# The MLP over two halves of 528 tokens in quarters of 264 columns, all sixteen pairs by seven products

## The chip, the cores and the metric

The kernel runs on one core of one Trainium2 chip. The metric is the device time of one launch in microseconds (us), lower is better. Three runs of the kernel before gave 1785.30, 1794.46 and 1788.88 us, median 1788.88.

## The reference

One step of a hybrid encoder layer on 1024 prompt tokens and 32 tokens of a second request, 1056 in all, with D = 1024 and weights shared by both. In float32 throughout:

```python
h = rms_norm(x, g_mix); q, k, v, ch, cb, cc, ga, gb = split(h @ w_in)
x = x + (sigmoid(ga) * (attn(q, k, v) @ w_attn_out) + sigmoid(gb) * (cb * conv3(cc * ch) @ w_conv_out)) @ w_mix_out
cq = rms_norm(x, g_cross) @ w_cq                  # 4 heads of 64, 256 memory tokens
x = x + (softmax(cq mem_k / 8) mem_v) @ w_co
x = x + square(relu(rms_norm(x, g_mlp) @ w_up)) @ w_down      # w_up 1024 x 4096, w_down 4096 x 1024
y = rms_norm(x, g_final)
```

The last line but one, the MLP, is what the change rewrites.

## The kernel before

Activations are held transposed: a tile is 128 features (partitions) by tokens (columns), and `x1[c][f]` is slice f (of eight) of token chunk c. The three chunks `CH` have 384, 384 and 288 tokens. Every float32 product is three matmuls on values split in a high part (fp32r) and the rest: weight-high by activation-high, weight-high by activation-low, weight-low by activation-high (`gemm` L183 to L185, `product` L851 to L853, `part` L1586 to L1588). The weights are the 128x128 stationary operand and the tokens the moving one, so a matmul costs by its columns.

A weight of 512 KB (128 x 1024) is loaded by SyncE into `wr` (two buffers), cast on ScalarE to `wh` (L125) and the difference `wl` taken on VectorE (L126), with three buffers of `wh` and `wl` and two weights of lead (`LOOK`). SP issues nearly all DMAs, in the order in which the Python code runs. Work is laid down by hand as a list of items (`item`, `beside`): `beside` lays one step of a list (attention work) and some late calls after each filler. A weight in `kept` has its low part stored the first time (`wl_d`), and read back the second time. Instructions of an engine run in the order in which the built program has them; PSUM tiles `acc`, `pa` and `pq` are released by the engine that reads them.

The part that matters here comes after the mix projection of the last chunk:

- Cross-attention of chunk 2 goes in steps beside fillers (`cross_steps(2)`). Fillers are MLP products: the first eight of 32 slices of w_up by chunk 0, then the same eight by chunk 1 (`do_up`, 24 matmuls of 384 columns each, L183 to L185), then the same eight by chunk 2 (288 columns). `normed_split` makes the normalised operand of a chunk: a product with gain and `R[c]` (L1212), a write to `xn_d`, a cast (L1215) and a subtraction (L1216); R comes from the statistics (`chunk_stats`, L214 to L242), and of chunk 1 it comes while the fillers on chunk 0 run. `up_part` evicts a result: relu (L1240 or L1242), a square on GpSimd (L1244), a write of the hidden slice.
- `combine` (L1263 to L1273) makes the sums t2, n1, n3, n4 of the operands of chunk 0 and chunk 1, four features each, on VectorE, ScalarE and GpSimd, beside the products of chunk 2. They are the left operands of a Strassen-like scheme.
- The remaining 24 slices of w_up go as 12 pairs (`up_pair`). The tokens of chunks 0 and 1 are the two halves of the scheme, and a pair of weight slices gives the four results (two halves by two slices) in seven products of half the depth, instead of eight. `pair_issue` makes the weight sums on GpSimd (L1292 to L1295). Chunk 2 goes the plain way (`up_c2`, tile `pa`). Each pair takes 84 matmuls of 384 columns and 48 of 288. The results are combined on VectorE (h22 L1368 and L1369, u2 L1359, h12 L1378, h21 L1393, m3 and m2 at L1383 and L1386) and on GpSimd (n1 L1388, m4 L1396), squared (L1320) and stored in DRAM.
- `open_down` and the down projection: seven products per pair again on 384 columns for chunks 0 and 1, with chunk 2 plain beside them (`beside_two`, `alone`, `two`). Operands that the four plain fillers made are combined later by `refold` (reads, subtractions and writes of their own); operands come through `pump` (load, cast L781, subtraction L782) before they are due. `final` and `final_last` make the final norm and write the output.

The tail after the last product is the last chunk's addition, its statistics and transposes (L1636), and the scaling and writing of the transposed output (L1652, L1654).

Of the kernel before, what the change touches and what calls it, by code (L numbers as in the profile page):

```python
# [23 lines left out]
NF = 8  # L24
KV = 4
# [13 lines left out]
def hybrid_step(ctx: ExitStack, tc: tile.TileContext, io):  # L39
# [40 lines left out]
    xn_d = [dram.tile([P, NF, n], F32, name=f"xn_d{c}") for c, (_, n) in enumerate(CH[:2])]  # L80

    op_d = {k: dram.tile([P, 16, 384], F32, name=f"{k}_d") for k in ("b11", "b12", "b21", "b22", "n1", "n3", "t2", "n4")}
    hid2_d = dram.tile([P, 2, 16, 288], F32, name="hid2_d")
# [671 lines left out]
    def yslot(c):  # L755
        return slot(Y["pool" if c < 2 else "top"], f"Y{c}", CH[c][1])
# [11 lines left out]
    def open_y(*_):  # L768
        closed(A["cm"])
        closed(kv_cm)  # L770
        G["pool"] = ctx.enter_context(tc.tile_pool(name="gb", bufs=5, reuse_waits="tile", side="right"))
        Y["pool"] = ctx.enter_context(tc.tile_pool(name="ypool", bufs=16, reuse_waits="tile", side="right"))
        open_top()
# [91 lines left out]
    def close_gates():  # L865
        pump(0)
        assert not wanted
        closed(Y["cm"])
        open_top()
        ctx.push(Y["cm"])  # L870
# [124 lines left out]
    mpool = cr_cm = cr = None  # L995

    def after_gates():
        nonlocal mpool, cr_cm, cr
# [4 lines left out]
        mpool = ctx.enter_context(tc.tile_pool(name="mpool", bufs=16, reuse_waits="tile"))  # L1003
        cr_cm, cr = opened("cross", bufs=1, reuse_waits="tile")
# [7 lines left out]
    xm = [[None] * NF for _ in CH]  # L1012
# [160 lines left out]
    def do_co(c, half):  # L1173
        def fn(w):
# [3 lines left out]
            for f in fs:  # L1178
# [9 lines left out]
                if half == 0 and c == 2:  # L1188
                    xm[c][f] = gain_split(x, G_MLP + f, c)
                square_acc(x, f, c)  # L1190
            if half == 1 and c == 2:
                for f in fs:
                    xm[c][f] = gain_split(x1[c][f], G_MLP + f, c)
# [7 lines left out]
    L = {}  # L1201

    def open_late():
        closed(cr_cm)
        L["cm"], L["pool"] = opened("late", bufs=1, reuse_waits="tile")

    def lt(n=384):
        return L["pool"].tile([P, n], F32, tag="lt", bufs=6, name=nm("lt"))

    def normed_split(c, f):  # L1210
        t = tmp(CH[c][1])
        pin(dve.scalar_tensor_tensor(t, x1[c][f], col(G_MLP + f), R[c], op0=ALU.mult, op1=ALU.mult))  # L1212
        sp.dma_start(xn_d[c][:, f], t)
        hi, lo = xm[c][f] = (yslot(c), yslot(c))
        act.copy(hi, t)  # L1215
        pin(dve.tensor_sub(lo, t, hi.bitcast(F32)))  # L1216
# [12 lines left out]
    def hidden(c, j, h):  # L1229
        half, i = j % 8 // 4, j // 8 * 4 + j % 4  # L1230
        put(hid2_d[:, half, i] if c == 2 else op_d[f"b{half + 1}{c + 1}"][:, i], h)

    def up_part(w, c, j):
        n = CH[c][1]
        a = ps.tile([P, n], F32, tag="pt", bufs=2, name=nm("pa")) if w[0] == "late" else acc_tile([P, n])
        gemm(a, w[-2:], xm[c])
        flush()
        t = tmp(n)
        if c == 2:
            dve.scalar_tensor_tensor(t, a, 0.0, R[c], op0=ALU.max, op1=ALU.mult)  # L1240
        else:
            dve.tensor_scalar_max(t, a, 0.0)  # L1242
        h = tmp(n)
        pool_e.tensor_tensor(h, t, t, op=ALU.mult)  # L1244
        hidden(c, j, h)

    def do_up(j, c):
        return (lambda w: up_part(w, c, j)), ("w_up", j)
# [4 lines left out]
    def comb_slot(kind, k):  # L1253
        if kind in ("N1", "N3"):
            return mslot(384)
        return L["pool"].tile([P, 384], F32R, tag="hx", bufs=8, name=nm("hx")) if k < 2 else yslot(1)

    def combine(k):
        b12, b22, b11, b21 = (lt() for _ in range(4))
        for t, c, f in ((b12, 1, k), (b22, 1, k + 4), (b11, 0, k), (b21, 0, k + 4)):  # L1260
            sp.dma_start(t, xn_d[c][:, f])
        n3, n1, t2, n4 = b22, b12, b11, b21
        pin(dve.tensor_sub(n3, b12, b22))  # L1263
        pin(dve.tensor_sub(n1, b11, b12))
        pin(dve.tensor_sub(t2, b11, n3))
        pin(pool_e.tensor_tensor(n4, b21, t2, op=ALU.subtract))
        for kind, x in (("T2", t2), ("N1", n1), ("N3", n3), ("N4", n4)):
            hi, lo = comb[kind, k] = (comb_slot(kind, k), comb_slot(kind, k))
            act.copy(hi, x)
            if kind[0] == "T" or kind == "N1":  # L1270
                pin(dve.tensor_sub(lo, x, hi.bitcast(F32)))
            else:
                pin(pool_e.tensor_tensor(lo, x, hi.bitcast(F32), op=ALU.subtract))  # L1273
# [5 lines left out]
    def pair_fetch(key, src1, src2):  # L1279
        r1 = wp.tile([P, 1024], F32, tag="wr", bufs=2, name=nm("wr"))  # L1280
        r2 = L["pool"].tile([P, 1024], F32, tag="wr2", bufs=2, name=nm("wr2"))
        sp.dma_start(r1, src1)
        sp.dma_start(r2, src2)
        raws[key] = [r1, r2]

    def pair_issue(key, which):
        r1, r2 = raws[key][:2]
        a, b = slice(0, 512), slice(512, 1024)
        if which == 4:
            s31 = L["pool"].tile([P, 1024], F32, tag="s31", name=nm("s31"))  # L1290
            s24 = L["pool"].tile([P, 1024], F32, tag="s24", name=nm("s24"))
            pool_e.tensor_tensor(s31[:, b], r2[:, a], r2[:, b], op=ALU.add)  # L1292
            pool_e.tensor_tensor(s24[:, a], r1[:, a], s31[:, b], op=ALU.add)
            pool_e.tensor_tensor(s24[:, b], r1[:, b], s24[:, a], op=ALU.add)
            pool_e.tensor_tensor(s31[:, a], r1[:, a], r2[:, a], op=ALU.add)  # L1295
            raws[key] += [s31, s24]
        src = {1: 0, 2: 1, 3: 2, 4: 3}[which]
        if which == 2:
            hi, lo = (L["pool"].tile([P, 1024], F32R, tag=t, name=nm(t)) for t in ("wh2", "wl2"))
        else:  # L1300
            hi, lo = (wp.tile([P, 1024], F32R, tag=t, name=nm(t)) for t in ("wh", "wl"))
        split(hi, lo, raws[key][src])
        wset[key, which] = (hi, lo)

    UP = [(8 * g + i, 8 * g + i + 4) for g in range(1, 4) for i in range(4)]

    def up_fetch(i):
        if i < len(UP):
            pair_fetch(("u", i), io["w_up"][UP[i][0]], io["w_up"][UP[i][1]])

    def up_issue(i, which):
        if i < len(UP):
            pair_issue(("u", i), which)
        elif which != 2:
            if worder[wpos[0]] is STOP:
                wpos[0] += 1
            issue_w()

    def square_relu(v):
        dve.scalar_tensor_tensor(v, v, 0.0, v, op0=ALU.max, op1=ALU.mult)  # L1320
        return v

    b11, b21, b22 = (lambda k: xm[0][k]), (lambda k: xm[0][k + 4]), (lambda k: xm[1][k + 4])
    four = lambda get: [get(k) for k in range(4)]
    s1s, rs = {}, {}

    def up_w(i, which):
        return wset[("u", i), which]

    def up_p1(i):  # L1330

        A = acc_tile([P, 384])
        product(A, up_w(i, 1), 0, four(b11), True)
# [506 lines left out]
```

## Time and profile before

| | us |
|---|---|
| runs | 1785.30, 1794.46, 1788.88 (median 1788.88) |
| the profiled execution's span | 1791.7 |
| end of the last mix product, start of the fillers | 1057.2 |
| first matmul of the pairs | 1176.9 |
| first matmul of the down projection | 1435.6 |
| last addition of chunk 1 after the last product | 1779.4 |

Besides its span the profiled execution has no time of its own on the page; the span lies 2.8 us above the median of the runs and within their spread. One row of "lines" gives engine, operation, output and inputs, shapes and number of instructions, then the busy time and mean duration, then the idle time of that engine ahead of them. A window's row gives its length and each engine's busy time (instructions in parentheses), then the granted TensorE clock, the DMA engines' mean share, and GB/s. A row of the timeline gives the start, the duration, the engine, the line and the operation, with the idle time before it and its releaser in brackets. A matmul's own duration is longer than the distance to the next one, since they overlap; that distance is what counts. A row of DMA issues gives the queue's engine, number, size and the median us from issue to landing.

### The profile page before, as it was taken

The page shows a single profiled execution, that of the slowest core. Times are in us where ns is not written, and L with a number is a line of the kernel's source. Part 1 is how long each engine was busy: PE and PEld are TensorE (multiplying, and loading weights), DVE is VectorE, ACT ScalarE, POOL GpSimd, SP SyncE. Part 2 cuts the span into 40 slices and gives each one's busy share as a digit, 9 for nine tenths or more (in the row PEclk, how much of TensorE's full clock was granted, in tenths as well). Part 3 has the DMA queues.
Part 4 walks back from the last instruction along what each step waited for, and adds up shares of the span by engine and source line. Part 5 has one row for each costly group of instructions (what it writes and reads, how often), then busy time and mean ns, then how long its engine had stood idle before and what let it go on. Part 6 is the DMA issues. An engine that isn't in the chain of part 4 may idle for free. (4 is left out here: it accounts for less than half of the span.)

```text
span 1791.7 us, 30247 instructions
## 1 busy us (share of the span) xinstructions
PE 1754.1 (98%) x11110; PEld 1732.5 (97%) x11110; DVE 1173.1 (65%) x2165; ACT 799.6 (45%) x1566; POOL 594.2 (33%) x681
## 2 busy tenths in 40 slices
PE   8999999999999999999999989999999999999997
PEld 8999999999999999999999989999999999999997
DVE  6776767868666646546566777767566676436763
ACT  8643534435345334334565745632222343324453
POOL 0013146553453444511224142386554300100111
PEclk9999999999999999999999999999999999999999
DMA  5232234344346888758765657754333487446673
GB/s 181 98 116 92 87 104 153 118 142 144 137 151 239 286 281 282 270 196 274 261 208 201 229 187 252 254 180 148 131 127 137 150 291 246 144 131 214 198 234 125
DMA packets 183858, 331.50 MB, mean 185 GB/s; under 512 B 18768, under 2 KB 139376, under 8 KB 183584
## 3 DMA queue, kind: packets, MB, share of 16 engines
q1 hardware_dynamic: 169936, 281.18, 46.7%
q0 software_dynamic: 13776, 48.41, 7.6%
q8 instruction: 87, 1.43, 0.3%
q14 instruction: 59, 0.48, 0.1%
HBM read 242.99 MB, written 86.52 MB: 184 GB/s over the span
## 5 line engine op out<-in xcount | busy, mean ns | idle before, releaser
L126 DVE TENSOR_TENSOR wl<-wr,wh 128x1024 fp32r<-128x1024 f32 x225 | 300.9, 1337 | 178.6 <-ACT wh L125 175.8
L125 ACT CAST wh<-wr 128x1024 fp32r<-128x1024 f32 x225 | 236.8, 1052 | 401.1 <-PE acc L1587 103.1
L183 PE MATMUL acc<-X,wh 128*128 128x384 f32 (+1 forms) x864 | 282.2, 327 | 8.2 <-ACT wh L125 8.2
L184 PE MATMUL acc<-X,wh 128*128 128x384 f32 (+1 forms) x864 | 279.4, 323 | 0.0
L185 PE MATMUL acc<-X,wl 128*128 128x384 f32 (+1 forms) x864 | 278.9, 323 | 0.3 <-DVE wl L126 0.3
L183 PE MATMUL acc<-Y,wh 128*128 128x384 f32 (+1 forms) x624 | 201.9, 325 | 0.8 <-DVE ct L1242 0.3
L185 PE MATMUL acc<-Y,wl 128*128 128x384 f32 (+1 forms) x624 | 202.1, 324 | 0.0
L184 PE MATMUL acc<-Y,wh 128*128 128x384 f32 (+1 forms) x624 | 201.7, 324 | 0.0
L259 POOL TENSOR_TENSOR xacc<-xacc,ct 128x384 f32<-128x384 f32 (+1 forms) x62 | 75.4, 1218 | 339.8 <-ACT ct L257 334.2
L183 PEld LDWEIGHTS acc<-X,wh 128*128 128x128 f32 x864 | 163.2, 189 | 8.8 <-ACT wh L125 8.2
L184 PEld LDWEIGHTS acc<-X,wh 128*128 128x128 f32 x864 | 163.5, 189 | 0.6
L185 PEld LDWEIGHTS acc<-X,wl 128*128 128x128 f32 x864 | 163.1, 189 | 0.8 <-DVE wl L126 0.8
L183 PEld LDWEIGHTS acc<-Y,wh 128*128 128x128 f32 x624 | 117.4, 189 | 1.8 <-DVE ct L1089 0.6
L185 PEld LDWEIGHTS acc<-Y,wl 128*128 128x128 f32 x624 | 117.8, 189 | 0.0
L184 PEld LDWEIGHTS acc<-Y,wh 128*128 128x128 f32 x624 | 117.7, 189 | 0.0
L1586 PE MATMUL acc<-Y,wh 128*128 128x384 f32 (+1 forms) x352 | 112.7, 322 | 1.1 <-DVE lt L1378 0.7
L1587 PE MATMUL acc<-Y,wh 128*128 128x384 f32 (+1 forms) x352 | 113.1, 321 | 0.0
L1588 PE MATMUL acc<-Y,wl 128*128 128x384 f32 (+1 forms) x352 | 112.8, 321 | 0.0
L125 ACT CAST PTh<-pt 128x512 fp32r<-128x512 f32 (+3 forms) x94 | 46.2, 517 | 115.8 <-PE pt L572 107.8
L707 POOL TENSOR_TENSOR xacc<-xacc 128x256 f32<-128x256 f32 x92 | 83.7, 909 | 4.9
L851 PE MATMUL acc<-Y,wh 128*128 128x384 f32 x248 | 83.1, 336 | 1.8 <-ACT wh L125 1.8
L1244 POOL TENSOR_TENSOR ct<-ct 128x288 f32<-128x288 f32 (+1 forms) x48 | 45.2, 943 | 116.7 <-DVE ct L1240 45.7
(360 smaller groups left out, 4759.5 us busy)
## 6 DMA issues: line engine op xcount, KB each, us to landing
wr<-in_w_in SPq DMA_DIRECT2D x53, 512.0 KB, 3.5
wr<-in_w_up SPq DMA_DIRECT2D x48, 512.0 KB, 4.0
wr<-in_w_down SPq DMA_DIRECT2D x32, 512.0 KB, 4.0
wr<-wsum_d SPq DMA_DIRECT2D x32, 512.0 KB, 3.9
wl<-wl_d SPq DMA_DIRECT2D x28, 512.0 KB, 4.6
wr<-in_w_conv_out SPq DMA_DIRECT2D x24, 512.0 KB, 4.4
wr<-in_w_mix SPq DMA_DIRECT2D x24, 512.0 KB, 4.4
ct<-b_d SPq DMA_DIRECT2D x48, 192.0 KB, 4.1
```

Source lines behind the costliest of these rows:

```text
L125: act.copy(hi, src)
L126: dve.tensor_sub(lo, src, hi.bitcast(F32))
L183: pe.matmul(out, wh[:, a], hi, start=(k == 0), stop=False)
L184: pe.matmul(out, wh[:, a], lo, start=False, stop=False)
L185: pe.matmul(out, wl[:, a], hi, start=False, stop=(k == len(acts) - 1))
L259: pool_e.tensor_tensor(acc, acc, sq, op=ALU.add)
L707: pin(pool_e.tensor_tensor(t[:, to], t[:, x], t[:, y], op=ALU.add))
L851: pe.matmul(acc, wh[:, a], hi, start=(start and k == 0), stop=False, skip_group_check=True)
L1244: pool_e.tensor_tensor(h, t, t, op=ALU.mult)
L1586: pe.matmul(a, wh[:, s], hi, start=(start and k == 0), stop=False, skip_group_check=True)
L1587: pe.matmul(a, wh[:, s], lo, start=False, stop=False, skip_group_check=True)
L1588: pe.matmul(a, wl[:, s], hi, start=False, stop=(stop and k == len(acts) - 1), skip_group_check=True)
```

## The change

Tokens are taken as two halves of 528 (`HT`), the second starting inside chunk 1, and each half as two quarters of 264 (`QT`) so that a bank of PSUM holds a quarter. All 16 pairs of slices go by seven products; chunk 2 has no products of its own. A pair has 120 matmuls, all of 264 columns. The product s1 = b11 by the first half-depth of the first slice, and the result b11, of all 16 pairs, are made ahead as fillers: for the first six pairs one quarter at a time (`up_one`, one weight each, so that these weights are loaded twice), for the other ten both quarters in two fillers (`up_two`). Both are stored in DRAM (`s1_d`, `op_d["b11"]`) and read back in the pair (`up_load`). The operands of the second quarter are read back from `xn_d` and split (`second_load`, `second_split`), since they stem from two chunks; the sums are made from loads of 528 columns (`comb_load`, `comb_sums`). In the pairs the four weight sums are made one pair ahead (`up_sums`, one buffer each for s31 and s24) and the first product of the next pair stands inside the present one (`up_t2`). The down projection has eight stages of eight weights (`stage`): seven kinds of operands, each weight followed by 48 matmuls of 264 columns, and the last kind, b22, in two passes of 24 matmuls a weight, one for each quarter. `pump2` loads operands straight into the low tile and splits them there. Chunk 0 is finished during stage n1, chunk 1 during the last pass, and chunk 2 at the end (`final_last`). `refold`, `combine` and the plain products are gone.

The core of the diff, the new lines (the removed functions stand in the section on the kernel):

```diff
+    def normed(c, f):
         t = tmp(CH[c][1])
         pin(dve.scalar_tensor_tensor(t, x1[c][f], col(G_MLP + f), R[c], op0=ALU.mult, op1=ALU.mult))
+        for h, to, at in in_halves(c):
+            sp.dma_start(xn_d[h][:, f, to], t[:, at])
+        if c == 0:
+            hi, lo = (yslot(0)[:, :QT] for _ in range(2))
+            xa[0][f] = (hi, lo)
+            act.copy(hi, t[:, :QT])
+            pin(dve.tensor_sub(lo, t[:, :QT], hi.bitcast(F32)))
+
+    def split_here(hi, lo):
+        raw = lo.bitcast(F32)
+        pin(act.copy(hi, raw))
+        pin(dve.tensor_sub(lo, raw, hi.bitcast(F32)))
+
+    def second_load(f):
+        z = zslot()
+        xa[1][f] = (quarter(z, 0), quarter(z, 1))
+        sp.dma_start(xa[1][f][1].bitcast(F32), xn_d[0][:, f, QT:])
+
+    def second_split(f):
+        split_here(*xa[1][f])
...
+    def up_one(i, q):
+        def fn(w):
+            flush()
+            a, b = (acc_tile([P, QT]) for _ in range(2))
+            s, h = lslot(), lslot()
+            product(a, w, 0, xa[q][:4], True)
+            s, h = s[:, :QT], h[:, :QT]
+            act.copy(s, a)
+            put(quarter(s1_d[:, i], q), s)
+            product(b, w, 1, xa[q][4:], True)
+            dve.tensor_add(h, b, s)
+            act.activation(h, h, AF.Relu)
+            pool_e.tensor_tensor(h, h, h, op=ALU.mult)
+            put(quarter(op_d["b11"][:, i], q), h)
+        return fn, ("w_up", UP[i][0])
...
+    def comb_sums(k):
+        both = xacc_tile()
+        n3, n1 = both[:, :HT], both[:, HT:]
+        t2, n4 = lslot(), lslot()
+        pin(dve.tensor_sub(n3, raw("n1", k), raw("n3", k)))
+        pin(dve.tensor_sub(t2, raw("t2", k), n3))
+        pin(dve.tensor_sub(n1, raw("t2", k), raw("n1", k)))
+        pin(pool_e.tensor_tensor(n4, raw("n4", k), t2, op=ALU.subtract))
+        for kind, x in (("t2", t2), ("n1", n1), ("n3", n3), ("n4", n4)):
+            hi, lo = comb[kind, k]
+            pin(act.copy(hi, x))
+            pin(dve.tensor_sub(lo, x, hi.bitcast(F32)))
...
+    def up_pair(i):
+        last = i == len(UP) - 1
+        s1, h11 = held[i]
+        c = [ps.tile([P, 512], F32, tag="pt", bufs=2, name=nm("pc"))[:, :QT] for _ in range(2)]
+        doubled(c, wset[i, 3], 1, "n1", True)
+        up_issue(i, 2)
...
+        doubled(banks_of(B[i]), wset[i, 3], 0, "n3", False)
+        h22 = lt()
+        dve.tensor_sub(quarters(h22), B[i][:, :, :QT], quarters(s1))
+        for q in range(2):
+            dve.tensor_sub(quarter(h22, q), quarter(h22, q), c[q])
+        squared_relu(h22)
+        put(op_d["b22"][:, i], h22)
...
+            up_issue(i + 1, 4)
+            up_t2(i + 1)
+            up_issue(i + 1, 3)
+        if i + 2 < len(UP):
+            up_fetch(i + 2)
+            up_sums(i + 2)
+        flush()
+        doubled(c, wset[i, 4], 1, "b22", False)
+        h12 = u2s.pop(i)
+        for q in range(2):
+            dve.tensor_sub(quarter(h12, q), c[q], quarter(h12, q))
+        squared_relu(h12)
+        m3, m2 = lt(), lt()
+        dve.tensor_sub(m3, h12, h22)
+        put(op_d["n3"][:, i], m3)
+        dve.tensor_sub(m2, h11, m3)
+        put(op_d["t2"][:, i], m2)
+        pool_e.tensor_tensor(h12, h11, h12, op=ALU.subtract)
+        put(op_d["n1"][:, i], h12)
...
+        doubled(banks_of(B[i]), wset[i, 2], 1, "n4", False)
+        h21 = s1
+        dve.tensor_sub(quarters(h21), B[i][:, :, :QT], quarters(s1))
+        squared_relu(h21)
+        put(op_d["b21"][:, i], h21)
+        m4 = h11
+        pool_e.tensor_tensor(m4, h21, m2, op=ALU.subtract)
+        put(op_d["n4"][:, i], m4)
...
+    def pump2(n):
+        for hi, lo in coming2:
+            split_here(hi, lo)
+        coming2.clear()
+        for kind, k in wanted2[:n]:
+            hi, lo = dn[kind, k] = dslots(kind, k)
+            sp.dma_start(lo.bitcast(F32), op_d[kind][:, k])
+            coming2.append((hi, lo))
+        del wanted2[:n]
...
-    for name, n in (("w_conv_out", NF), ("w_mix", NF), ("w_cq", 2), ("w_co", 2), ("w_up", NF)):
+    for name, n in (("w_conv_out", NF), ("w_mix", NF), ("w_cq", 2), ("w_co", 2)):
...
+    NQ = 6
+    fillers = [up_one(i, q) for q in range(2) for i in range(NQ)]
+    for i in range(NQ, len(UP)):
+        fillers += up_two(i)
+    late = [(f // 2, lambda f=f: normed(1, f)) for f in range(NF)]
+    late += [(3 + f // 4, lambda f=f: second_load(f)) for f in range(NF)]
+    late += [(4 + f // 4, lambda f=f: second_split(f)) for f in range(NF)]
+    steps = left + cross_steps(2)
+    at = len(steps)
+    late.append((at, open_sums))
+    late += [(at + f // 4, lambda f=f: normed(2, f)) for f in range(NF)]
+    late.append((at + 1, lambda: comb_load(["t2", "n4"])))
+    late.append((at + 2, lambda: comb_load(["n3", "n1"])))
+    late += [(at + 4 + 2 * k, lambda k=k: comb_sums(k)) for k in range(4)]
+    late.append((at + 4, lambda: up_fetch(0)))
+    late.append((at + 7, lambda: up_sums(0)))
+    late.append((at + 9, lambda: up_fetch(1)))
+    left = beside(steps, fillers, late)
...
+    for i in range(len(UP)):
+        item(lambda i=i: up_pair(i))
...
+    stage("b11", ("w_down", 0), ((*A12, True, False), (*A21, False, False), (*A22, False, False), (*A11, True, False)))
+    stage("b21", ("w_down", 1), ((*A11, True, True),))
+    stage("n4", ("w_down", 3), ((*A21, True, False),))
+    stage("t2", ("w_sum", 0), ((*A12, False, False), (*A21, True, False), (*A22, True, False)))
+    stage("n3", ("w_sum", 2), ((*A21, True, True), (*A22, True, False)))
+    stage("n1", ("w_sum", 3), ((*A22, False, True), (*A12, True, False)), more=lambda: final(0))
+    item(lambda: gained(2, range(4, 8)))
+    stage("b22", ("w_sum", 1), ((*A12, True, True),), q=0)
+    stage("b22", ("w_sum", 1), ((*A12, True, True),), q=1, more=lambda: final(1),
+          each=lambda j: gained(2, [j]) if j < 3 else None)
+    item(lambda: final_last(2))
```

More of the change, by code (lines that the diff above doesn't have):

```diff
@@ L1247, in do_up @@
-    def do_up(j, c):
-        return (lambda w: up_part(w, c, j)), ("w_up", j)
-    comb = {}
[L1253 to L1273, printed above, removed]
+    UP = [(8 * g + i, 8 * g + i + 4) for g in range(4) for i in range(4)]
@@ L1594, in fn, with banks_for, prod @@
+    def banks_for(j, q):
+        if q is None:
+            return banks_of(wide_tile())
+        if j % 2 == 0:
+            bank["pair"] = wide_tile()
+        one = bank["pair"][:, j % 2, :QT]
+        return [one, None] if q == 0 else [None, one]
+    def prod(kind, j, t, then, q=None):
         def fn(w):
[L1595 to L1597 removed]
+            if t == 0:
+                bank[j] = banks_for(j, q)
+            part(bank[j], w, kind, t)
```

513 lines of the change are left out of this document (213 added, 300 removed).

## The prediction

> **What bounds the kernel now.** I read the page's share by engine first, then its busy slices, then the windows of the three MLP stages (the span is the 1791.7 us of the page's head).
>
> ```profile
> PE 1754.1 (98%) x11110; PEld 1732.5 (97%) x11110; DVE 1173.1 (65%) x2165; ACT 799.6 (45%) x1566; POOL 594.2 (33%) x681
> ...
> PE   8999999999999999999999989999999999999997
> ...
> 1058.00:1177.00 119.00, 115.38 (x752) 113.61 (x751) 87.23 (x160) 67.89 (x137) 41.31 (x39) 1.00 0.73 251
> 1200.00:1420.00 220.00, 219.67 (x1376) 219.35 (x1376) 137.43 (x173) 54.53 (x62) 117.76 (x95) 1.00 0.40 134
> 1436.00:1779.00 343.00, 340.85 (x2127) 336.95 (x2126) 198.72 (x322) 143.29 (x249) 27.73 (x22) 1.00 0.62 200
> ```
>
> TensorE is busy 98% and in every slice but the ends; the granted clock is 1.00 in all three stages. No other engine is near it: VectorE has 73% in the stage with the fillers (1058 to 1177), 62% in the pairs. So TensorE's work is the time, as long as the others keep feeding it, and a change is priced by matmuls times start-to-start distance, plus the stalls it makes or removes. The distances come from the timeline:
>
> ```profile
> 1134.78 0.28 PE L1156 MATMUL o<-PTh,mv 128*128 128x256 f32 x1
> ...
> 1135.25 0.29 PE L1183 MATMUL acc<-Y,wh 128*128 128x288 f32 x1
> ...
> 1135.52 0.29 PE L1185 MATMUL acc<-Y,wl 128*128 128x288 f32 x1
> 1136.76 0.53 PE L1183 MATMUL acc<-Y,wh 128*128 128x288 f32 x2 [0.95 <-ACT Y L1165]
> ...
> 1280.28 0.34 PE L851 MATMUL acc<-hx,wh 128*128 128x384 f32 x1
> ...
> 1284.45 0.29 PE L183 MATMUL pa<-Y,wh 128*128 128x288 f32 x1
> ...
> 1297.30 0.29 PE L183 MATMUL pa<-Y,wh 128*128 128x288 f32 x1
> ...
> 1299.94 0.29 PE L185 MATMUL pa<-Y,wl 128*128 128x288 f32 x1
> ```
>
> Four matmuls of 256 columns lie between the first two rows: 0.1175 us each. Two products, 24 matmuls of 384, lie between 1280.28 and 1284.45: 0.1738 each. Twenty steps of 288 lie between the last two: 0.132 each. The line through 288 and 384 gives 0.118 at 256, so it holds there too, and 0.1216 at 264 columns, a size that the trace does not have. The bounds are 0.1175 (the 256 row) and 0.132 (the 288 row); 264 is nearest to 256, and I take the line.
>
> **The work.** Counted in the two programs, the change removes 2734 matmuls of 384 columns and 1538 of 288 and adds 5376 of 264: all 16 pairs go by seven products, where before four of them and a third chunk of 288 tokens were done in full, and 1104 more, narrower matmuls pay for it. 2734 x 0.1738 = 475.2, 1538 x 0.132 = 203.0, 5376 x 0.1216 = 653.7: TensorE's work falls by 24.5 us. At the 256 row's distance it would fall by 46.5; at the 288 row's it would grow by 31.5.
>
> [...]
>
> **The filler stage.** Here the change puts new round trips through DRAM on the path. The rows for it:
>
> ```profile
> 1057.22 0.34 PE L183 MATMUL acc<-Y,wh 128*128 128x384 f32 x1
> ...
> 1071.47 0.62 DVE L1212 SCALAR_TENSOR_TENSOR ct<-Ga,prm,R 128x384 f32<-128x384 f32 x1 [0.30 <-ACT st_s L217]
> 1072.59 1.23 DVE L126 TENSOR_TENSOR wl<-wr,wh 128x1024 fp32r<-128x1024 f32 x1
> ...
> L1212 DVE SCALAR_TENSOR_TENSOR ct<-Ga,prm,R 128x384 f32<-128x384 f32 x3 | 3.0, 998 | 0.3 <-ACT st_s L217 0.3
> ...
> wr<-in_w_up SPq DMA_DIRECT2D x48, 512.0 KB, 4.0
> xn_d<-ct SPq DMA_DIRECT2D x16, 192.0 KB, 2.8
> lt<-xn_d SPq DMA_DIRECT2D x16, 192.0 KB, 5.0
> ...
> 1153.40 0.77 PE L214 MATMUL pq<-ones,xacc 128*128 128x1 f32 x6
> 1160.53 0.40 ACT L242 COPY R<-pr 128x288 f32<-128x288 f32 x1 [0.89 <-PE pr L232]
> ...
> L125 ACT CAST wh<-wr 128x1024 fp32r<-128x1024 f32 x18 | 19.0, 1053 | 16.9 <-PE acc L184 7.6 <-DMA wr<-in_w_up 6.8 <-PE acc L185 2.5
> ...
> 1174.75 0.30 PE L184 MATMUL acc<-Y,wh 128*128 128x288 f32 x1
> 1176.85 0.44 PE L851 MATMUL acc<-Y,wh 128*128 128x384 f32 x1 [1.80 <-ACT wh L125]
> ```
>
> Before, the fillers begin at 1057.22 on chunk 0 and go over to chunk 1 without a gap, since its operands are split where they are made. Starts further apart than the distances above sum to 9 us from there to the steady pairs, 2 of them at 1174.75 and 1.1 at 1135.52.
>
> After, the second quarter (tokens 264 to 527) has tokens of both chunks, so it is written to xn_d, read back and split again. The built order lays 25.6 us of TensorE's work between the stage's start and the first product of that quarter (six fillers of 24 x 0.1216 = 2.92, the rest attention and statistics): it comes due at 1082.8. Chunk 1's R is there at 1071.47; eight norm products and the weight splits between them take about 11 us at 0.62 to 0.998 and 1.23, then 2.8 for the write, 5.0 for the read and about 1 for cast and split: 1091. Stall 8; 4 if the first four slices are enough to start, 13 if the norm products all wait for POOL. The reads wait on SP with the next weights queued behind, and ACT's casts wait with the next weights' casts behind: 1 us. With two buffers a weight takes 4.0 to land, 1.05 to cast and 1.23 to subtract, 6.3 / 2 = 3.15 us, against 2.92 in the first fillers; attention steps between them cover that.
>
> Then the sums t2, n1, n3, n4, now of 528 columns. From chunk 2's statistics to the first product that needs them stand 35 us of TensorE's work. R takes 7.5 us (1153.40 to 1160.93 for the same chunk), the five products that the first sums need 2.8 (0.55 each, between 288/384 of 0.62 and of 0.998), write and read 7.8: the first sum can start at 18. Then 25 subtractions stand in VectorE's order before the last split of t2, with four weight splits (5.4 at about 1.34, between L126's 1.23 and the 1.57 below).
>
> ```profile
> L1263 DVE TENSOR_TENSOR lt<-lt,lt 128x384 f32<-128x384 f32 x2 | 1.2, 605 | 0.0
> ...
> L1271 DVE TENSOR_TENSOR M<-lt,M 128x384 fp32r<-128x384 f32 x2 | 2.7, 1365 | 0.0
> ...
> L126 DVE TENSOR_TENSOR wl<-wr,wh 128x1024 fp32r<-128x1024 f32 x21 | 32.9, 1567 | 1.7 <-ACT wh L125 1.7
> L126 DVE TENSOR_TENSOR wl<-s,wh 128x1024 fp32r<-128x1024 f32 x22 | 27.8, 1263 | 5.0 <-ACT wh L125 5.0
> L1386 DVE TENSOR_TENSOR lt<-xacc,lt 128x384 f32<-128x384 f32 x11 | 14.4, 1311 | 0.7
> ...
> L1383 DVE TENSOR_TENSOR lt<-lt,lt 128x384 f32<-128x384 f32 x11 | 6.0, 550 | 0.0
> ...
> L1293 POOL TENSOR_TENSOR s<-wr,s 128x512 f32<-128x512 f32 x11 | 21.4, 1942 | 0.0
> ...
> L1295 POOL TENSOR_TENSOR s<-wr,wr 128x512 f32<-128x512 f32 x10 | 17.1, 1714 | 0.0
> L1388 POOL TENSOR_TENSOR lt<-xacc,lt 128x384 f32<-128x384 f32 x11 | 15.4, 1404 | 6.3 <-issue 4.7 <-DVE lt L1383 1.6
> L1292 POOL TENSOR_TENSOR s<-wr 128x512 f32<-128x512 f32 x10 | 15.4, 1542 | 44.1 <-DVE wl L126 44.1
> L1294 POOL TENSOR_TENSOR s<-wr,s 128x512 f32<-128x512 f32 x11 | 14.4, 1306 | 0.1
> L1396 POOL TENSOR_TENSOR lt<-lt,lt 128x384 f32<-128x384 f32 x11 | 11.1, 1013 | 1.0 <-DVE lt L1320 1.0
> ```
>
> One of 384 columns takes 0.55 alone (L1383) and 1.31 to 1.37 beside POOL (L1386, L1271); scaled to 528, about 0.72 and 1.88. POOL now has fewer of these sums (one of seven steps instead of three of eight), so I take 0.95: 18 + 25 x 0.95 + 5.4 = 47, less 35 is a stall of 12; all free 6, all held 35. Attention's output products (1.1 us at 1135.52) and the other small gaps keep about 4 us. The stage then loses 8 + 1 + 12 + 4 = 25 against 9: +16.
>
> [...]
>
> **The pairs.** A pair has 120 matmuls, 14.59 us. VectorE does three weight splits and nine passes, five of 528 columns and four of 264: 3 x 1.34 + 5 x 0.72 + 4 x 0.43 = 9.3 us; POOL 6.5 for the four sums and 3.3 for n1 and m4 (1.404 and 1.013 at 384 columns, times 528/384); 3.2 MB move in 14.59 us, 219 GB/s, below the 251 of the filler stage. What could bind is a chain through s31 and s24, of which there is one buffer each: h22 (0.72 + 2 x 0.43), split of w3 1.26, the four sums 6.5, cast 1.05, split of w4 1.26, m2 0.72 to 1.8, then the next h22: 12.4 to 13.5 us, under 14.59. So +1 for the sixteen pairs.
>
> **Down.** The row at the change of stages:
>
> ```profile
> 1435.64 0.41 PE L1586 MATMUL acc<-Y,wh 128*128 128x384 f32 x1 [0.74 <-DVE lt L1378]
> ```
>
> Before, the first down stage waits for VectorE's last passes over PSUM in the pairs; starts further apart than the distances sum to 5 us between 1429 and 1450, this wait among them. After, b11 was stored some 100 us before it is read; I leave 2: -3. The last operand, b22, goes in two passes of 2.92 us a weight against a supply of 3.15; the lead of two weights hides most, +1. The tail after the last product is the same kind of chain.
>
> **Sum.** -24.5 + 16 + 1 - 3 + 1 = -9.5. The profiled execution's span of 1791.7 becomes 1782; it lies 2.8 above the median of the runs, so 1779 is the time against 1788.88. With the distance and stall bounds weighted to the near ends, this case's own range is 1768 to 1790.
>
> **The rivals.**
> *All hidden* (0.12): the reads land early and TensorE stays ahead. VectorE's 73% in the old stage leaves room for it. The stage stays at 9: 1791.7 - 25.5 - 2.8 = 1763.
> *The pair chain binds* (0.13). If all meet POOL: h22 1.58, splits 1.57 + 1.57 or up to 1.85, sums at 1.94 each 7.76, cast 1.05, m2 1.8, about 15.9 us. It decides from 14.59 on, and costs 1.3 x 15 = 20 us: 1779 + 20 = 1799, about at the edge of slower. For it: L1293's 1.94 and L1386's 1.31. Against: the sums' 6.5 are already measured beside VectorE.
> *VectorE held in the sums* (0.15), the slower side: each of the 25 subtractions at 1.88, the stall 35 instead of 12: 1802. It is slower than before by over the bound from about 1.7 us each. For it: L1271's 1.365. Against: POOL is free of most splits.
> *The narrow matmul costs what 288 columns cost* (0.05): the change does not save TensorE's work; 24.5 becomes -31.5: 1835.
> The forecast itself has 0.55.
>
> **How the numbers follow.** About 0.5% (9 us) is what a measurement of this kernel can tell from no change: faster is below 1780, slower above 1798. Of the forecast's 0.55, 0.32 fall below 1780 and 0.22 within, 0.01 above; all hidden adds 0.12 to faster; the pair chain is half same, half slower; the held sums give 0.04 same and 0.11 slower, the narrow matmul 0.01 and 0.04. That is 0.44 faster, 0.33 same, 0.23 slower. The range from 1763 to 1802 takes in the first rival and stops at the held sums, leaving out about 0.15.
>
> **What would show it.** Distances of 264-column matmuls near 0.1216; two waits of TensorE on second-quarter operands (released by the split from Z, about 8 us) and before the first t2 product (about 12 us); in the pairs, 14.6 us from one h22 to the next; the first down stage with no wait over 1 us. It is wrong if the pairs take over 15 us each, if TensorE waits less than 5 us or more than 30 in the filler stage, or if the distance is not within 0.118 to 0.126.

## The result, and the profile after

The changed kernel takes 1801.2 us (median of five, 1796.26 to 1802.02) where the kernel before takes 1791.83 (five runs): ratio 1.0046, 95% interval 1.0024 to 1.0068; the medians lie 9.4 us apart, the changed kernel the slower one. The forecast was 1779, 10 us faster. The range of 1763 to 1802 holds the time, at its very end; the direction was wrong.

The page of the changed kernel, the share by engine, then two of the rows of 40 slices (a digit is the busy share, or the granted clock, in tenths):

```profile
span 1799.4 us, 32416 instructions
PE 1743.8 (97%) x12214; PEld 1722.0 (96%) x12214; DVE 1185.3 (66%) x2215; ACT 851.1 (47%) x1648; POOL 596.9 (33%) x659
...
PE   8999999999999999999999989979999999999997
...
PEclk9999999999999999999999989989999999999999
```

TensorE is busy 10.3 us less than before in a span that is 7.7 us longer, and the slice with the 7 (1170 to 1215), new against the row before, is where the sums lie. The 8 ahead of it stood there before too. Windows of the changed kernel: the fillers of the first stretch, the stretch of the sums, the pairs, and 20 us near the end.

```profile
1058.00:1110.00 52.00, 44.87 (x320) 43.22 (x318) 34.02 (x68) 30.71 (x67) 12.82 (x13) 0.90 0.74 228
1110.00:1222.00 112.00, 98.12 (x747) 95.79 (x746) 80.69 (x121) 61.68 (x141) 44.42 (x34) 0.94 0.63 214
...
1222.00:1420.00 198.00, 198.00 (x1627) 198.00 (x1626) 130.05 (x163) 91.76 (x123) 116.08 (x81) 1.00 0.67 216
...
1736.00:1756.00 20.00, 17.01 (x109) 15.98 (x108) 9.49 (x15) 6.65 (x9) 3.23 (x3) 0.83 0.40 126
```

The same first stretch of the kernel before:

```profile
1058.00:1110.00 52.00, 51.36 (x316) 50.81 (x315) 38.43 (x71) 26.95 (x54) 13.31 (x11) 1.00 0.71 243
```

TensorE loses 7 of 52 us there, with a granted clock of 0.90 for 1.00, and no other engine is full. The pairs lose nothing: 198.00 busy of 198.00. Their period is read from the timeline, VectorE's first pass of h22:

```profile
1305.69 0.71 DVE L1431 TENSOR_TENSOR Z<-acc,lt 128x528 f32<-128x528 f32 x1 [1.52 <-PE acc L856]
1320.32 0.71 DVE L1431 TENSOR_TENSOR Z<-acc,lt 128x528 f32<-128x528 f32 x1 [1.52 <-PE acc L856]
1334.94 0.71 DVE L1431 TENSOR_TENSOR Z<-acc,lt 128x528 f32<-128x528 f32 x1 [1.53 <-PE acc L856]
```

14.63 and 14.62 us for 120 matmuls, 0.1219 us each, and VectorE waits for TensorE, not the reverse. TensorE's waits in the changed kernel, 1057 to 1225:

```profile
PE acc L854 <- ACT lt L1310: 10.1, 3, 5.6
PE pr L233 <- ACT ct L231: 3.4, 1, 3.4
PE acc L854 <- ACT wh L127: 3.3, 3, 2.1
PE acc L856 <- DVE wl L128: 3.1, 3, 1.4
...
PE acc L855 <- DVE Z L1258: 0.3, 1, 0.3
```

The second quarter's split (Z), on which a wait of 8 us was forecast, holds TensorE for 0.3 us. The largest wait is for L1310, ScalarE's copy of a filler's half-product out of PSUM, which the next product needs.

Where the time went, worked out from the traces: for each stretch the sum, over all matmuls, of the distance to the next start less the prediction's line (6.6 ns and 0.4355 ns a column), in us. The hundred or so narrower matmuls (1 to 128 columns) do not follow that line: by the median they start 0.11 us apart in both kernels, where it gives 0.007 to 0.062. How they are priced moves a figure by up to 3 us, most in the last column, and the difference between the two kernels by under 2.

| kernel | 1057 to 1110 | to 1230 | to 1420 | to 1470 | to 1700 | to the end |
|---|---|---|---|---|---|---|
| before | 2.0 | 7.9 | 0.4 | 4.9 | 1.2 | 3.5 |
| changed | 13.6 | 22.6 | 0.5 | 6.2 | 0.7 | 10.2 |
| a1 (sums early) | 14.3 | 17.1 | 0.5 | 6.0 | 1.1 | 10.9 |
| a2 (second quarter early) | 10.9 | 23.8 | 0.5 | 6.1 | 1.1 | 10.3 |
| e3 (three operands) | 14.1 | 24.0 | 0.5 | 4.8 | 0.6 | 5.0 |
| f1 (direct sums) | 12.9 | 15.8 | 0.5 | 6.3 | 0.7 | 8.9 |
| f3 (both, three operands) | 12.3 | 16.8 | 0.5 | 4.0 | 0.9 | 4.7 |
| h1 (f3, third raw buffer) | 7.7 | 16.0 | 0.5 | 4.8 | 0.9 | 4.6 |

The changed kernel loses 33.9 us more than before; less the 24.5 us of work saved that makes 9.4 us slower. The two profiled executions, from which this is worked out, end 7.7 us apart, so the account closes to within 2 us.

How the waits come about is seen in the timeline. First stretch of the changed kernel (only the rows of one chain):

```profile
1072.21 0.33 SPq L147 DMA_DIRECT2D wr<-in_w_up  x1
...
1076.34 1.04 ACT L127 CAST wh<-wr 128x1024 fp32r<-128x1024 f32 x1 [3.65 <-DMA wr<-in_w_up]
...
1077.30 0.90 ACT L231 ACTIVATE ct<-ident,rc 128x128 fp32r<-128x128 f32 x3
...
1078.25 0.61 PE L233 MATMUL pr<-ct,ones_r 128*128 128x288 f32 x1 [3.37 <-ACT ct L231]
...
1097.77 0.59 PE L854 MATMUL acc<-Z,wh 128*128 128x264 f32 x1 [2.07 <-ACT wh L127]
```

A weight is issued at 1072.21, when a raw buffer comes free, and lands 4.1 us later; ScalarE's cast waits for it, the statistics' scaling (L231) stands behind that cast, and TensorE behind the scaling. At 1097.77 it waits for a weight directly. Then the sums, same kernel:

```profile
1170.64 3.17 SPq L1336 DMA_DIRECT2D n<-xn_d  x6
...
1173.99 0.71 DVE L1345 TENSOR_TENSOR xacc<-n,n 128x528 f32<-128x528 f32 x1 [3.83 <-DMA n<-xn_d]
...
1174.80 0.67 SPq L147 DMA_DIRECT2D wr<-in_w_up  x1
...
1175.47 0.63 ACT L1351 CAST t<-lt 128x528 fp32r<-128x528 f32 x1 [8.67 <-DVE lt L1346]
...
1176.01 0.65 ACT L1310 COPY lt<-acc 128x264 f32<-128x264 f32 x2
...
1176.43 0.59 PE L854 MATMUL acc<-Y,wh 128*128 128x264 f32 x1 [5.59 <-ACT lt L1310]
1176.82 0.42 PE L855 MATMUL acc<-Y,wh 128*128 128x264 f32 x1
1177.04 0.42 PE L856 MATMUL acc<-Y,wl 128*128 128x264 f32 x1
```

Six reads of chunk 2's operands hold SP's queue; VectorE waits 3.83 us for them, ScalarE 8.67 for VectorE, and the copy L1310, whose product TensorE had finished by 1171, stands behind that cast. The next weight is issued only behind the reads. The last two rows show a further cost: matmuls behind the wait start 0.22 us apart, not 0.122.

### The profile page after: what moved, and what is told of

It reads as the page before. It is cut to its first block, busy times and chain, and to the rows that moved or that the text cites. A ratio compares the mean times of both kernels' runs of the same rounds, so it can differ in the third digit from the quotient of the medians.

```text
span 1799.4 us, 32416 instructions
## 1 busy us (share of the span) xinstructions
PE 1743.8 (97%) x12214; PEld 1722.0 (96%) x12214; DVE 1185.3 (66%) x2215; ACT 851.1 (47%) x1648; POOL 596.9 (33%) x659
## 4 chain that ended last, share of the span: by engine, by line
PE 85%; DMA 6%; DVE 4%; issue 2%; ACT 1%; SPq 1%; POOL 0%; DVEq 0%; ACTq 0%; POOLq 0%
PE acc L185 12%; PE acc L187 12%; PE acc L186 12%; PE acc L1640 6%; PE acc L1642 6%; PE acc L1641 6%; PE acc L854 5%; PE acc L856 5%; PE acc L855 5%; PE pc L856 2%; PE pc L855 2%; PE pc L854 2%; PE pt L574 2%; DVE wl L128 1%; DMA wr<-in_w_up 1%
## 5 line engine op out<-in xcount | busy, mean ns | idle before, releaser
L128 DVE TENSOR_TENSOR wl<-wr,wh 128x1024 fp32r<-128x1024 f32 x223 | 287.9, 1291 | 144.3 <-ACT wh L127 143.3
L261 POOL TENSOR_TENSOR xacc<-xacc,ct 128x384 f32<-128x384 f32 (+1 forms) x62 | 79.9, 1293 | 332.9 <-ACT ct L259 331.0
L185 PE MATMUL acc<-Y,wh 128*128 128x384 f32 (+1 forms) x432 | 138.8, 323 | 0.7 <-ACT Y L764 0.7
L186 PE MATMUL acc<-Y,wh 128*128 128x384 f32 (+1 forms) x432 | 139.3, 323 | 0.1
L187 PE MATMUL acc<-Y,wl 128*128 128x384 f32 (+1 forms) x432 | 139.3, 323 | 0.0
L1641 PE MATMUL acc<-n,wh 128*128 128x264 f32 x352 | 101.9, 289 | 2.2 <-DVE n L1258 2.2
L1640 PE MATMUL acc<-n,wh 128*128 128x264 f32 x352 | 101.4, 288 | 0.0
L1642 PE MATMUL acc<-n,wl 128*128 128x264 f32 x352 | 101.2, 288 | 0.0
L709 POOL TENSOR_TENSOR ws<-ws 128x256 f32<-128x256 f32 x92 | 81.6, 887 | 7.1 <-DMA ws<-in_w_down 1.9
L185 PEld LDWEIGHTS acc<-Y,wh 128*128 128x128 f32 x432 | 80.9, 188 | 1.1 <-ACT Y L764 1.1
L186 PEld LDWEIGHTS acc<-Y,wh 128*128 128x128 f32 x432 | 81.1, 188 | 0.4 <-DVE Y L765 0.4
L187 PEld LDWEIGHTS acc<-Y,wl 128*128 128x128 f32 x432 | 81.1, 188 | 0.0
L560 ACT ACTIVATE S<-S,nmx 128x257 f32<-128x257 f32 (+1 forms) x132 | 64.2, 488 | 18.7 <-DVE nmx L555 17.3
```

The source lines that it names most:

```text
L128: dve.tensor_sub(lo, src, hi.bitcast(F32))
L185: pe.matmul(out, wh[:, a], hi, start=(k == 0), stop=False)
L186: pe.matmul(out, wh[:, a], lo, start=False, stop=False)
L187: pe.matmul(out, wl[:, a], hi, start=False, stop=(k == len(acts) - 1))
L709: pin(pool_e.tensor_tensor(t[:, to], t[:, x], t[:, y], op=ALU.add))
L1640: pe.matmul(a, wh[:, s], hi, start=(t == 0 and k == 0), stop=False, skip_group_check=True)
```

## The experiments

Times are medians with the ratio to the kernel before, run on the same chip beside it. The diffs are shortened, and some of their lines tell in words what several lines of code do.

**Are the round trips the cause? (a1, a2)** Both leave the instructions and bytes and take away the waiting, with other data:

```diff
a1: -  comb_load(["t2","n4"]) at +1, ["n3","n1"] at +2, from xn_d[h]
    +  both ahead of normed(2), from xn_d[0]
a2: -  sp.dma_start(xa[1][f][1].bitcast(F32), xn_d[0][:, f, QT:])   # at 3 + f // 4
    +  sp.dma_start(xa[1][f][1].bitcast(F32), xn_d[0][:, f, :QT])   # at 0, ahead of normed(1)
```

> The sums t2, n1, n3, n4 are made from the first half's normalised operands alone (n1 and n3 read half 0 where they should read half 1), and these loads stand ahead of chunk 2's norm products in the order: the values are others, the instructions and bytes are the same, and nothing waits for the round trip of chunk 2 through DRAM. Theory A (round trip: ScalarE's casts for the sums wait for the late loads, and behind them in ScalarE's order stand the evictions that TensorE needs): TensorE's waits on L1310, 10.1 us of the changed kernel, fall under 2, time about 1792, that is 8 to 10 us under the changed kernel's 1801. Theory B (VectorE is held by GpSimd in the subtractions): the waits stay, time 1798 to 1801.

Measured 1792.56 us, ratio 0.9988 (0.9973 to 1.0002): level with before, as theory A had it. But the waits on L1310 fell from 10.1 to 7.1 us, not under 2, so the round trip is part of the stretch's loss (22.6 to 17.1), and the rest stays.

> The second quarter's operands are read from the first quarter's tokens (chunk 0 alone, stored long before), and their loads stand ahead of chunk 1's norm products: other values, same instructions and bytes, no wait for chunk 1's round trip. Theory A: the wait on the split from Z (4.2 us at 1091 to 1097) goes and perhaps part of the 3.4 us wait of the statistics at 1075, time 1794 to 1797. Theory B: no change, 1800 to 1801.

Measured 1797.19, ratio 1.0017 (1.0003 to 1.0031), at the upper end of theory A's numbers. The first stretch still loses 10.9 us, so most of its loss is not the second quarter's.

**Sums later in the order (a3, a4)**

```diff
-    late += [(at + 4 + 2 * k, lambda k=k: comb_sums(k)) for k in range(4)]
+    late += [(at + 5 + 2 * k, ...        # a3; a4: at + 6
```

> The four sums stand one filler later (at + 5 + 2k for at + 4 + 2k), so the casts for a sum stand behind the copy L1310 of the next filler, nothing else changes. Theory A: the 5.6 us wait at 1171 goes almost wholly, the two later ones (1.7 and 2.8) too, and up to 3 come back before the first t2 product: time 1793 to 1797. Theory B: VectorE's work is only put off, all of it comes due at the pairs' start: 1801 to 1804.

> The four sums stand two fillers later (at + 6 + 2k). Theory A: as one filler later at 1171, but the copy L1310 of the next filler but one stands behind the casts again, and the last sum is later: 1795 to 1799. Theory B: 1802 to 1806.

1804.73, ratio 1.0061 (1.0037 to 1.0084), and 1805.46, 1.0067 (1.0041 to 1.0093): theory A missed both, and they lie at theory B's upper end. The trace of a3:

```profile
1175.89 0.47 SPq L147 DMA_DIRECT2D wr<-in_w_up  x1
...
1182.23 1.04 ACT L127 CAST wh<-wr 128x1024 fp32r<-128x1024 f32 x1 [13.98 <-DMA wr<-in_w_up]
```

The sums no longer hold the copy; now a weight's cast holds the relu that empties a product (L1321), for the weight was issued at 1175.89, behind the reads. One queue's wait took the place of the other's. That the times came out near theory B's doesn't bear B out: VectorE stood idle 13 us behind that cast, not held in its subtractions.

**The reads off SP's queue, or later (e1, e2, e4)**

```diff
e1: -  sp.dma_start(lo.bitcast(F32), xn_d[h][:, f])
    +  (sp if kind == "b22" else pool_e).dma_start(lo.bitcast(F32), xn_d[h][:, f])
e2: e1 and second_load by pool_e;   e4: loads at + 3 and + 4, sums at + 6 + 2 * k
```

> The loads for the sums (comb_load without b22) are issued on GpSimd's queue instead of SyncE's, everything else as in the changed kernel. Theory C (SyncE's order: the reads wait on SP for the writes of chunk 2 to land, and the next weights stand behind them, so that they are issued some 5 us late): the weights are issued on time, the waits of TensorE between 1167 and 1205 fall by 5 us or more: 1793 to 1796. Theory A (ScalarE's order: casts wait for the sums however the loads are issued): the 5.6 us wait on L1310 stays, 1799 to 1801.

> As the run before, and the second quarter's loads (second_load) on GpSimd's queue too. Theory C: a further 2 to 3 us of the waits between 1075 and 1097, 1790 to 1794. Theory A: the wait on the split from Z stays as it is, no further change.

> The loads for the sums stand two fillers later in the order, and the sums two fillers later, so that the weights of two fillers stand ahead of the loads on SyncE's queue and the loads need not wait for chunk 2's writes. Theory C: no long wait on weights at 1171 to 1185, the rest as before: 1794 to 1798. Theory A: likewise 1796 to 1799. Theory B: all work is later, 1803 to 1806.

1806.89 (1.0071, 1.0050 to 1.0092), 1803.06 (1.0042, 1.0020 to 1.0065) and 1802.76 (1.0050, 1.0033 to 1.0067). None helped, all three lie above what theories A and C had forecast, and theory C by itself fell. In e1 the reads start at 1177.9, after the writes, so TensorE waits 13.6 us at one time for L1310 (15.2 in e2); in e4 SP still stands 4.6 us in the reads and ScalarE waits 10.2 us for the weight behind them. Wherever these reads were put, some queue waited behind them.

**No round trip (f1, f2)**

```diff
f1: +  if c == 2: sp.dma_start(raw(("n1","n3")[f // 4], f % 4)[:, 240:], t)   # from SBUF to SBUF
    +  t2, n4 and columns 0 to 239 of n1, n3 loaded early, each ahead of the normed(2) that fills the rest
    +  of chunk 2, only f >= 4 still written to xn_d
f2: +  if c == 1: hi, lo = (x[:, 120:] for x in xa[1][f]); act.copy(hi, t[:, :144])
    +             pin(dve.tensor_sub(lo, t[:, :144], hi.bitcast(F32)))
    +  only columns 0 to 119 of the second quarter read back, ahead of normed(1)
```

> A valid version: chunk 2's norm products go by one SBUF-to-SBUF DMA straight into the operands' tiles (columns 240 to 527 of n1 and n3), and only the first 240 columns, with t2 and n4, are loaded from DRAM, ahead of them on SyncE. One DMA landing instead of a write and a read on the chain, and no read that waits on SP for a write with the next weights behind. Theory D (the round trip holds SP and with it the weights, and by ScalarE's order the evictions; both end with the round trip): losses of the sums' stretch fall from 22.6 us to about 17, as with the early data, time 1793 to 1796. Theory A alone (ScalarE's order whatever the data): 1799 to 1801.

1791.6, ratio 1.0002 (0.9987 to 1.0017), a little better than expected; the stretch's loss falls from 22.6 to 15.8, about 17 having been expected. Theory D holds for the part that the round trip had made: SP issues the next weight at 1169.75 instead of 1174.80, and TensorE's waits on the copies fall from 10.1 to 6.7 us. It does not hold for the rest, as the waits of f1 in this stretch show, TensorE's and ScalarE's:

```profile
PE acc L854 <- ACT lt L1313: 6.7, 4, 2.8
ACT t L1355 <- DVE lt L1350: 8.5, 4, 3.4
```

The casts of the sums still wait for VectorE's subtractions, and the copies (L1313 here) still stand behind these casts. About half of what the stretch had lost over the kernel before stays.

> A valid version: the second quarter's part from chunk 1 is split where it is made (as chunk 0's first quarter is), and only chunk 0's 120 columns are read back, early. No wait on chunk 1's round trip. Theory D: the stretch from 1057 to 1110 loses about 10 instead of 13.6 us, time 1797 to 1799. If sixteen more small operations on ScalarE and VectorE cost as much: 1801.

1795.81, ratio 1.0026 (1.0013 to 1.0039), a little better than expected, though its interval meets the changed kernel's. The profiled execution is the slowest of the ten (1803.58 us), and in it the first stretch lost 13.5 us as before. With a2's 10.9 this says that the second quarter is not the main thing that holds the stretch.

**The down projection (e3)**

```diff
-                pump2(2)
+                pump2(3)
```

> In the down projection each step asks for three operands of the next stage instead of two, so that all sixteen are asked for after six steps of eight instead of at the last. If the losses at the stages' borders (6 us at 1440 to 1460 is not touched, 7 us at 1720 to 1760 is) come from operands that are asked for too late, the time falls by 2 to 4 us: 1797 to 1799. If they come from PSUM banks that VectorE's additions release late, no change: 1801.

1794.68, ratio 1.0005 (0.9991 to 1.0018), a gain of some 0.4%, more than expected. The waits from 1700 on, first the changed kernel, then e3:

```profile
PE acc L1640 <- DVE Ga L1624: 2.3, 3, 1.0
PE acc L1641 <- DVE b L1258: 1.7, 2, 1.1
```

```profile
PE acc L1640 <- DVE Ga L1624: 2.4, 3, 1.0
```

The wait on late operands (b) is gone, that on PSUM banks (L1624 is the addition that empties one) has stayed, and the stretch loses 5.0 us instead of 10.2.

**All three together (f3), and what is left (h1, i1, j1)**

> Both of these and three operands a step in the down projection. If the parts add up: 1801 less 6.5 (measured for the three operands) less 5 to 7 less 2 to 4, that is 1784 to 1788, faster than the kernel before (1792) by 0.3 to 0.4%. If the waits only move: 1793 to 1796.

1787.49, ratio 0.9974 (0.9963 to 0.9985): faster than both kernels, than the one before by 0.3%, and within what was expected if the parts add up. The parts' gains, 0.44%, 0.20% and 0.41% by their ratios, come to 1.05%; together they made 0.72%.

h1, i1 and j1 are edits of f3:

```diff
h1: +  a third buffer for raw weights, used for every third weight from open_first to open_sums
i1: +  casts and splits of a sum at + 5 + 2 * k, its subtractions at + 4 + 2 * k
j1: -  NQ = 6
    +  NQ = 8
```

> The version with both direct parts and three operands a step, and a third buffer for raw weights during the fillers (between the last mix and the sums). Theory E (weight supply: a first filler uses a weight for 2.92 us, and with two raw buffers one is ready every 3.65 us, from two issued at 1064.9 until the next issue at 1072.2 in the changed kernel): the waits between 1057 and 1110, 12 us in that version, fall by 4 to 7 us, time 1781 to 1784 beside 1787.5. Theory F (the order on ScalarE and the split operands keep TensorE waiting there, not the weights): 1786 to 1789.

1786.52, ratio 0.9964 (0.9951 to 0.9977). By time it is not told apart from f3, and it came out in theory F's numbers, not in E's. What the change did at its place is seen in the traces: windows of f3 and of h1, each with ScalarE's wait for weights between 1057 and 1110,

```profile
1058.00:1110.00 52.00, 45.53 (x332) 43.82 (x331) 37.43 (x83) 33.20 (x80) 13.31 (x12) 0.93 0.67 213
...
ACT wh L127 <- DMA wr<-in_w_up: 5.3, 3, 3.1
```

```profile
1058.00:1110.00 52.00, 48.05 (x378) 46.34 (x377) 42.81 (x91) 36.98 (x92) 17.08 (x15) 1.00 0.81 246
...
ACT wh L128 <- DMA wr<-in_w_up: 0.6, 1, 0.6
```

TensorE's busy time rises by 2.5 us, the clock to 1.00, VectorE and the DMAs do more in the same 52 us, ScalarE's wait for weights all but ends, and the loss falls from 12.3 to 7.7. Theory E is borne out there by the traces, not by the time; the profiled execution of h1 is the fastest of its five. The other 5.7 us over the kernel before stay open.

> The version with both direct parts and three operands a step, with the casts and splits of each sum one filler behind its subtractions, so that the copies L1310 of the next filler stand ahead of the casts on ScalarE. Theory A' (what is left of TensorE's waits on the copies, 6.7 us in four, is ScalarE's order alone): they fall under 2 us, time 1782 to 1785. If VectorE's order holds the casts' sums anyway: 1786 to 1790.

1790.41, ratio 0.9990 (0.9980 to 0.9999), 0.16% above f3, with intervals that just meet, and no gain. TensorE's waits on the copies (6.8 us) did go, but in their place it waited 9.6 us, in five pieces, for the relu that empties the product before, which now stands behind the casts:

```profile
PE acc L854 <- ACT lt L1328: 9.6, 5, 4.0
```

It is ScalarE's order still, and moving the casts within that order only chooses which eviction waits.

> The version with both direct parts and three operands a step, with eight pairs instead of six whose first-half products go a quarter at a time: two more weights are loaded and split, four more fillers use a weight for 2.92 us alone, and the second quarter comes due 5.8 us later. Theory E: 1 to 3 us more, 1788 to 1791. If the second quarter is still what TensorE waits for: 1784 to 1786.

1787.8, ratio 0.9976 (0.9965 to 0.9987), level with f3, a little under theory E's range; it tells nothing apart.

**Slow matmuls behind a wait (g1)**

```diff
+            if i == 12:    # second() of up_two: 4 products of 12 matmuls into a bank that nobody reads
```

> 48 matmuls more of 264 columns, whose result nobody reads, stand ahead of the filler that waits longest (5.6 us at 1171 in the changed kernel), about 5.8 us of TensorE's work in place of the wait. If the slow spacing (0.22 us instead of 0.1216 for some 12 matmuls) behind a wait comes from TensorE's idling, the granted clock there stays at 1.00 and the slow matmuls are gone; the time is the same within noise. If it comes from something else that happens there (DMA traffic, VectorE), they stay slow.

One run, 1799.78: 5.8 us more of TensorE's work cost nothing that one run could show. But TensorE still waited at that place:

```profile
1179.68 0.59 PE L854 MATMUL acc<-Y,wh 128*128 128x264 f32 x1 [3.24 <-ACT lt L1310]
```

and 12 matmuls behind it ran slowly again, 1.2 us lost. Whether idling alone makes them slow was not settled by that place; two later waits of the same run say more, and stand in the last section.

## Why the prediction was wrong

**The work** was right. 264 columns take 0.1219 us against the estimate of 0.1216, and the saving of 24.5 us closes the account above to within 2 us. What failed is the price of the stalls.

**The filler stage** failed: 25 us forecast, 36.2 measured, and of its terms hardly one for the reason given.
- *Z, 8 us.* Measured 0.3. The term that stood in its place was the weights' supply, put at nothing because "attention steps between them cover that". It was taken as 3.15 us a weight with the median landing. Here two weights issued from 1064.9 on give up a buffer only at 1072.2, 3.65 us each, against 2.92 of work; TensorE's waits behind it are the 3.4 us on L231 and 3.0 of those on the weight's cast. h1 shows it as cause for some 4.6 us. The round trip itself was timed about right: the split operands were there from 1089 to 1093.5, for 1091 forecast. But TensorE came to the first of them only at 1089.31, for 1082.8 forecast, held before by the weights and by slow matmuls, so the earlier stall hid this one:

```profile
1089.31 0.28 PE L854 MATMUL acc<-Z,wh 128*128 128x264 f32 x1
```

- *The sums, 12 us.* The subtractions were priced at 0.95 us for VectorE. The rows:

```profile
L1352 DVE TENSOR_TENSOR n<-xacc,n 128x528 fp32r<-128x528 f32 x8 | 5.3, 695 | 0.0
L1352 DVE TENSOR_TENSOR t<-lt,t 128x528 fp32r<-128x528 f32 x4 | 4.8, 1210 | 0.1
...
L1345 DVE TENSOR_TENSOR xacc<-n,n 128x528 f32<-128x528 f32 x4 | 3.7, 917 | 3.8 <-DMA n<-xn_d 3.8
```

  With the other twelve (9.2 us) the 28 take 23.0 us, 0.82 each: VectorE was faster than forecast, and the rival that had it held at 1.88 did not happen. The stall came from what is queued behind a waiting instruction, on SP the weights (the next one issued only at 1174.80), on ScalarE the copies that free PSUM (10.1 us of TensorE's waits), and it lies in the fillers, not before the first t2 product (1.35 us there). The prediction named both queues for the second quarter, at 1 us, and left them out for the sums. f1 shows the round trip as cause for 6.8 of the 14.7 us that this stretch lost over the kernel before; of the rest, the 6.7 us of waits on the copies go by ScalarE's order behind VectorE's sums, and the one run that took them away (i1) put others in their place.
- *Slow matmuls, not priced at all.* Of the 36.2 us, 23.4 are waits over 0.3 us, 10.3 are matmuls between 1.5 and 2.6 times their distance, mostly in the 3 us behind a wait. Before, these were 4.9 and 3.9.

**The pairs**: right. The chain through s31 and s24 did not bind, 0.1 us more than before for +1 forecast.

**Down**: -3 forecast, +1.3 measured. b11 was stored long before, but its slots come free only with the last pair's products, so the loads are late all the same (the step "b11 was stored ... before it is read" looked at the data and not at the buffers). SP's wait in these loads (1420 to 1460), and TensorE's for their splits:

```profile
SPq L1502 <- PE pc L856: 5.3, 2, 4.9
...
PE acc L1641 <- DVE n L1258: 2.2, 2, 1.3
```

No run moved these loads, so this is read from one trace.

**The last pass**: +1 forecast, +6.7 measured; two operands a step bring the last ones as they are due, and e3 shows 5.2 of it. That b22 with 24 matmuls a weight hides less was not tested.

Summed: 10 on the filler stage (26.3 more than before for 16), 4 and 6 in the down projection, less 1 in the pairs and 0.5 between the last two, is 19 us on the forecast of -9.5, which gives the 9.4 of the account. Of the 33.9 us that the changed kernel loses over the one before, the edits of f3 took away 14.6 and those of h1 19.3; the rest stays open.

That 1801.2 still lies inside the range is luck: it reached that far for two rivals that did not happen, the pair chain at 1799 and VectorE held in the sums at 1802. Nor did any of the signs of being wrong appear: a pair took 14.6 us, TensorE's waits in the filler stage came to 23.4 us, and the distance was 0.1219. No sign looked at the slow matmuls, at the last pass or at what the waits were for.

## What to carry to other kernels

A change that cuts the bounding engine's work by 25 us in 735 gains only if it keeps that engine fed as well as before; price each new wait by everything queued behind it on its engine and on the DMA queue, not by its own length: here VectorE's 3.83 us behind six reads stood in a chain with 8.67 on ScalarE and 5.59 on TensorE. Moving such a wait to another place or queue moved the loss (a3, a4, e1, e2, e4: 1802.8 to 1806.9 us); taking the round trip away removed about half of it (f1, 6.8 of 14.7 us). When a matmul gets narrower, check how many microseconds of work a weight buys against how long a buffer is held (here 2.92 of work, and a buffer free every 3.65).

## What the runs showed of the hardware

Behind some waits 12 to 15 matmuls of 264 columns in a row start some 0.22 us apart instead of 0.122, for some 3 us: five times between 1057 and 1222 in the changed kernel, 1.2 to 1.5 us lost each time. Windows of the changed kernel behind waits of 5.6, 1.7 and 2.8 us:

```profile
1176.00:1180.00 4.00, 3.57 (x18) 3.57 (x19) 3.54 (x5) 2.65 (x7) 1.22 (x1) 0.56 1.04 394
1186.30:1190.00 3.70, 3.62 (x17) 3.62 (x18) 3.70 (x4) 2.30 (x6) 0.87 (x1) 0.54 0.54 160
1201.40:1205.00 3.60, 3.59 (x29) 3.59 (x30) 3.60 (x4) 3.51 (x7) 0.81 (x1) 1.00 0.39 110
```

The granted clock was 0.56 and 0.54 behind the first two, and 1.00 behind the third, although that wait was longer than the second. g1 has the same two waits, of 1.7 and 2.8 us, some 4 us later, and there it is the other way round: full clock behind the first, half behind the second, from 1.1 us after its end on:

```profile
1190.50:1194.50 4.00, 3.90 (x32) 3.90 (x33) 4.00 (x5) 3.05 (x7) 0.89 (x1) 1.00 0.53 172
...
1206.60:1210.00 3.40, 3.40 (x18) 3.40 (x17) 3.40 (x6) 2.07 (x4) 0.00 (x0) 0.50 0.65 211
```

In these rows the mean granted clock is about half (0.50 to 0.56) or full (1.00), and the length of the wait does not decide which: a wait of 1.7 us had half behind it in the changed kernel and full in g1, one of 2.8 us the reverse. What decides it was not shown.
